# Log-keep sums of a stick-breaking attention: fp32r products of high and low parts in place of fp32 products

## The chip, the core and the metric

The kernel runs on one core of one Trainium2 chip. A core has a matrix engine (TensorE, PE in the profile, with its weight loads listed apart as PEld), three engines for elementwise work (VectorE or DVE, ScalarE or ACT, GpSimd or POOL) and SyncE (SP), which issues most transfers from HBM. Each engine works through its own queue in order and waits for others by semaphores. The metric is the device time of one execution in microseconds. Before the change it is 2654.6 us, the median of 3 runs (2654.39 to 2655.65).

## The reference, cut to what matters

The program is a decoder of two layers over 272 tokens (16 learned ones and 256 of input), width 2048: an RWKV-7 layer with a SwiGLU, then keys and values projected once, then a layer of stick-breaking attention with 16 heads of 128, and a second SwiGLU. The change is in the attention:

```python
z = jnp.einsum('bhqd,bhkd->bhqk', q_blk, k).astype(jnp.float32) * scale
log_keep = jnp.where(valid, -jax.nn.softplus(z), 0.0)
later = lax.cumsum(log_keep, axis=3, reverse=True) - log_keep
weights = jnp.where(valid, jnp.exp(jax.nn.log_sigmoid(z) + later), 0.0)
return jnp.einsum('bhqk,bhkd->bhqd', weights.astype(v.dtype), v)
```

For each query and key, `later` is the sum of the log-keep values of all keys that come after this key (and before the query). The kernel computes these sums as matrix products.

## The kernel before, in words

Activations lie transposed, features on the 128 partitions and tokens along the free axis. Every large projection splits its weights and its activations into a high part, rounded to the narrower type fp32r, and a low part, the remainder, also in fp32r, and adds three products of such parts. Weights stream in through `parts` (lines 152 to 172): SP loads a tile `raw`, ScalarE copies 128x512 of it to `whi` (line 170), VectorE subtracts to get `wlo` (line 171), and six of each may be in flight. In `mm3k` (lines 185 to 194) the matrix engine multiplies them, for the attention's query projection with one matmul of 256 columns (line 193) and one of 512 (line 194) per block of 128 rows.

`attention` (line 987) first makes the keys and values of all 16 heads, then runs `attn_head` (line 1034) for the heads through `interleave` (line 617). That loop takes turns between several heads: `attn_head` is a generator, each `yield` ends a turn, and a new head starts every second turn. The order of instructions on each engine follows from these turns and from the scheduler of the framework, which is free to move instructions within an engine here (the layer before is fixed by hand, the attention isn't).

For one head, `attn_head` does, in this order:

- the query projection, 16 blocks (`mm`, 32 matmuls); then the copy `c` (line 203) on ScalarE and `qx` (lines 204 and 205) on VectorE;
- `head_norm` (line 965): squares `hsq` (line 969), their parts `hs` (lines 971 on ScalarE and 972 on VectorE), two fp32r matmuls `hms` (line 975), an inverse root `hy` and `ht` (lines 978 to 984), and the normed query `q` (line 985);
- the transposed values `tbv` (line 1046) and their copy `vt` (line 1048);
- the scores `z` (line 1054, three fp32 products of 256, 144 and 16 columns);
- on ScalarE and VectorE the log-keep `lk` (lines 1057 to 1062), 128 keys on the partitions by 416 columns of three blocks of keys, and `e`, the log of the sigmoid (line 1063);
- the sums over later keys, `lt` (lines 1065 to 1071);
- `e` plus `lt` (line 1073, VectorE), its exponential (line 1074, ScalarE), the mask (line 1075, VectorE);
- the weighted values `op` (lines 1078 to 1080, three fp32 products), the copy `o` (line 1083) and its parts `hl`.

The sums `lt` take three products that accumulate in one PSUM bank: a triangular matrix of ones times all 416 columns, a full matrix of ones times columns 256 to 400 (144), and the same times columns 400 to 416, written twice (32). The matrices and `lk` are fp32 here, and the profile shows two matmul records for each of the three. GpSimd has no work in the attention: its last work is the recursion for the RWKV layer (lines 1274 to 1281), whose last subtraction starts at 583.6 us.

Of the kernel before, what the change touches and what calls it, by code (L numbers as in the profile page):

```python
# [11 lines left out]
F32 = mybir.dt.float32  # L12
F32R = mybir.dt.float32r
AF = mybir.ActivationFunctionType
ALU = mybir.AluOpType
# [106 lines left out]
class Builder:  # L122
# [864 lines left out]
    def attention(self):  # L987
        tc, nc, a = self.tc, self.nc, self.a
        rs = self.rs
        with ExitStack() as ctx:  # L990
            self.pre = tc.keep_in_program_order(
                nc.scalar.preload_act_table_set("natural_log_exp_and_others"))
            self.at = at = ctx.enter_context(tc.tile_pool(name="at", bufs=2))
            self.ones = at.tile([128, 128], F32R, name="ones", tag="ones", bufs=1)
            nc.scalar.copy(self.ones, self.cst("ones128"))
            Ks, Vs = [], []
            xs = []

            def key_norm(m):
                kv = self.kr.tile([128, 2 * T], F32, name="kv", tag="hl")  # L1000
                k = kv[:, :T]
                Vs.append(kv[:, T:])
                self.head_norm(xs[m], T, self.kgain, k)
                self.dump("K", m, k)
                Ks.append(k)

            first = self.proj_pair((a["sb_w_k"][0], a["sb_w_k"][1]), self.hx2)
            for m in range(NK):
                ps = first[m] if m < 2 else self.proj(a["sb_w_k"][m], self.hx2)
                x = at.tile([128, T], F32, name="kx", tag="kx", bufs=3)  # L1010
                nc.vector.tensor_tensor(x, ps, rs, ALU.mult)
                xs.append(x)
                if m > 0:
                    key_norm(m - 1)
            key_norm(NK - 1)
            for m in range(NK):
                ps = self.proj(a["sb_w_v"][m], self.hx2)
                nc.vector.tensor_tensor(Vs[m], ps, rs, ALU.mult)
                self.dump("V", m, Vs[m])
            os = [None] * NK  # L1020
            self.wide = False
            self.interleave(lambda m: self.attn_head(m, Ks[m], Vs[m], rs, os), ASTRIDE)
            self.wide = True
            acts = []
            for m in range(NK):
                ps = self.proj(a["sb_w_o"][m], os)
                h = self.h[m]
                self.added(h[:, META:], ps)
                self.dump("h3", m, h[:, META:])
                acts.append(self.finish_h(m, META, m == 0, [("g_ffn1", META, self.xs2)])[0])  # L1030
            self.hx = acts
            self.rs = self.norm_rstd(META)

    def attn_head(self, m, K, Vv, rs, os):
        nc, a, at = self.nc, self.a, self.at
        PE, V, A = nc.tensor, nc.vector, nc.scalar
        ps = yield from self.proj_steps(a["sb_w_q"][m], self.hx3, ASTEP)
        x = at.tile([128, T], F32, name="qx", tag="kx", bufs=3)
        self.scaled(x[:, :SEQ], ps, rs[:, META:])
        q = at.tile([128, SEQ], F32, name="q", tag="q")  # L1040
        self.head_norm(x[:, :SEQ], SEQ, self.qgain, q)
        yield 1

        tb = self.pfr.tile([128, 512], F32, name="tbv", tag="fr")
        for i, o in enumerate((0, 128, 144)):
            PE.transpose(tb[:, i * 128:i * 128 + 128], Vv[:, o:o + 128], self.cst("ident"))
        vt = at.tile([128, 384], F32, name="vt", tag="vt")
        A.copy(vt, tb[:, :384])
        parts = ((0, 256, 0, 0), (256, 400, 112, 128), (400, 416, 240, 144))
        yield 1  # L1050
        n = 416
        z = self.psc.tile([128, 512], F32, name="z", tag="sc")
        for c0, c1, q0, k0 in parts:
            PE.matmul(z[:, c0:c1], K[:, k0:k0 + 128], q[:, q0:], start=True, stop=True)  # L1054
        yield 1
        e = at.tile([128, n], F32, name="e", tag="e")
        A.activation(e, z[:, :n], AF.Abs)
        A.activation(e, e, AF.Exp, scale=-1.0)
        A.activation(e, e, AF.Ln, bias=self.one)
        lk = at.tile([128, n], F32, name="lk", tag="lk")  # L1060
        V.scalar_tensor_tensor(lk, z[:, :n], 0.0, e, ALU.max, ALU.add)
        V.tensor_tensor(lk, lk, self.cst("nmask"), ALU.mult)
        V.scalar_tensor_tensor(e, z[:, :n], 0.0, e, ALU.min, ALU.subtract)
        yield 1
        lt = self.psd.tile([128, 512], F32, name="lt", tag="sd")
        tri, ones = self.cst("tri"), self.cst("ones")
        PE.matmul(lt[:, :n], tri, lk, start=True, stop=False)  # L1067
        PE.matmul(lt[:, 112:256], ones, lk[:, 256:400], start=False, stop=False)
        two = lt[:, 112:400].rearrange("p (a t) -> p a t", a=2)[:, :, 128:144]
        PE.matmul(two, ones, lk[:, 400:416].unsqueeze(1).to_broadcast([128, 2, 16]),  # L1070
                  start=False, stop=True)
        yield 1
        V.tensor_tensor(e, e, lt[:, :n], ALU.add)
        A.activation(e, e, AF.Exp)
        V.scalar_tensor_tensor(e, e, -1.0, self.cst("nmask"), ALU.mult, ALU.mult)
        yield 1
        op = self.psd.tile([128, 512], F32, name="op", tag="sd")
        PE.matmul(op[:, :SEQ], vt[:, 0:128], e[:, 0:256], start=True, stop=False)
        PE.matmul(op[:, 112:SEQ], vt[:, 128:256], e[:, 256:400], start=False, stop=False)
        PE.matmul(op[:, 240:SEQ], vt[:, 256:384], e[:, 400:416], start=False, stop=True)  # L1080
        yield 1
        o = at.tile([128, SEQ], F32, name="o", tag="o")
        A.copy(o, op[:, :SEQ])
        self.dump("ao", m, o)
        os[m] = self.split(o, self.xs1)
# [428 lines left out]
```

## Time and profile before

| what | value |
|---|---|
| median of 3 runs | 2654.6 us |
| the profiled execution's own time | 2656.68 us |
| its span, from first to last instruction | 2654.9 us |
| busy in the span: PE, DVE, ACT, POOL | 2641.9, 1787.6, 1490.5, 174.1 us |
| the 16 heads of the attention | about 1684 to 1835 us of the span |
| in these 151 us busy: PE, DVE, ACT, POOL | 151.00, 124.66, 116.62, 0.00 us |
| granted TensorE clock over the span | 1.000 of full |

A row of the timeline gives the start in us from the span's start, the duration in us, the engine, the line of the kernel, the operation, out<-in by tile names with shapes, and how many instructions were merged; a bracket gives the idle time of the engine before the row and what ended it. Matmuls are pipelined, so their durations overlap; what a matmul costs the engine is the time from its start to the next one's start.

### The profile page before, as it was taken

Reading aid. Unit: us, or ns where it says so; the run is one execution under the profiler, and the core shown is the slowest. Engines: PE = TensorE matmul, PEld = TensorE weight load, DVE = VectorE, ACT = ScalarE, POOL = GpSimd, SP = SyncE. Lnnn points to the kernel's source line nnn. Section 1 sums busy time; section 2 is a strip of 40 time slices with the busy share of each in tenths; the row PEclk is TensorE's granted clock in tenths of the full one; section 3 lists DMA queues with packets and bytes.
Section 4 is the critical chain, followed back from the end, with each engine's and each line's share of the span. In section 5 each row is a group of like instructions: output and inputs, shape, how many; then the busy total and the mean of one; then the engine's idle time right before and its main releaser. Section 6 shows DMA issues by size and latency. Waiting matters only on the chain.

```text
span 2654.9 us, 54070 instructions
## 1 busy us (share of the span) xinstructions
PE 2641.9 (100%) x20966; PEld 2455.2 (92%) x20966; DVE 1787.6 (67%) x3618; ACT 1490.5 (56%) x3017; POOL 174.1 (7%) x493
## 2 busy tenths in 40 slices
PE   9999999999999999999999999999999999999999
PEld 8898888889999999999999999888888888888888
DVE  7677777766655555555557775788766666666665
ACT  7775666666544444444446764676555455554553
POOL 0014343440000000000000000000000000000000
PEclk9999999999999999999999999999999999999999
DMA  6434343445555555555555555434555655665655
GB/s 229 145 120 130 96 127 97 124 132 165 174 175 165 186 175 165 185 176 167 184 174 168 181 167 175 143 120 137 189 187 180 197 188 176 201 190 176 199 180 177
DMA packets 186385, 439.54 MB, mean 166 GB/s; under 512 B 58736, under 2 KB 89616, under 8 KB 186128
## 3 DMA queue, kind: packets, MB, share of 16 engines
q1 hardware_dynamic: 184784, 432.90, 51.9%
q8 instruction: 164, 2.69, 0.4%
q0 software_dynamic: 768, 2.23, 0.3%
q10 hardware_dynamic: 576, 0.96, 0.1%
q14 instruction: 93, 0.76, 0.1%
HBM read 430.28 MB, written 5.74 MB: 164 GB/s over the span
## 4 chain that ended last, share of the span: by engine, by line
PE 97%; DMA 1%; ACT 1%; issue 1%; DVE 0%; POOL 0%; SPq 0%; POOLq 0%; ACTq 0%
PE mm L194 23%; PE mm L189 17%; PE mm L191 17%; PE mm L190 17%; PE mm L193 12%; PE lr L587 1%; PE mm L488 1%; PE cb L1426 1%; PE zb L1363 1%; PE yb L1344 1%; PE wa L1374 1%; PE z L1054 1%; PE cb L1418 0%; PE lt L1067 0%; PE ba L1226 0%
## 5 line engine op out<-in xcount | busy, mean ns | idle before, releaser
L171 DVE TENSOR_TENSOR wlo<-raw,whi 128x512 fp32r<-128x512 f32 (+1 forms) x1432 | 968.0, 679 | 596.4 <-ACT whi L170 576.5
L170 ACT CAST whi<-raw 128x512 fp32r<-128x512 f32 (+1 forms) x1432 | 870.3, 610 | 841.2 <-PE mm L190 531.3
L189 PE MATMUL mm<-hl,whi 128*128 128x272 f32 x3328 | 967.2, 291 | 0.0
L191 PE MATMUL mm<-hl,wlo 128*128 128x272 f32 x3328 | 960.4, 289 | 0.0
L190 PE MATMUL mm<-hl,whi 128*128 128x272 f32 x3328 | 958.1, 288 | 0.0
L194 PE MATMUL mm<-hl,whi 128*128 128x512 f32 x2624 | 919.9, 394 | 0.0
L193 PE MATMUL mm<-hl,wlo 128*128 128x256 f32 x2624 | 738.1, 282 | 0.0
L189 PEld LDWEIGHTS mm<-hl,whi 128*128 128x128 f32 x3328 | 625.3, 188 | 10.7 <-issue 8.1
L190 PEld LDWEIGHTS mm<-hl,whi 128*128 128x128 f32 x3328 | 631.2, 190 | 0.0
L191 PEld LDWEIGHTS mm<-hl,wlo 128*128 128x128 f32 x3328 | 625.6, 188 | 0.2
L194 PEld LDWEIGHTS mm<-hl,whi 128*128 128x128 f32 x2624 | 492.4, 188 | 111.9
L193 PEld LDWEIGHTS mm<-hl,wlo 128*128 128x128 f32 x2624 | 494.3, 188 | 0.3
L218 DVE TENSOR_TENSOR wlo<-raw,whi 128x512 fp32r<-128x512 f32 (+2 forms) x156 | 106.6, 691 | 21.7 <-ACT whi L217 19.3
L217 ACT CAST whi<-raw 128x512 fp32r<-128x512 f32 (+2 forms) x156 | 93.1, 609 | 41.4 <-PE mm L190 40.9
L210 DVE TENSOR_TENSOR h<-h,mm 128x256 f32<-128x256 f32 (+1 forms) x224 | 93.9, 420 | 6.6 <-PE mm L194 6.0
L203 ACT COPY c<-mm 128x256 f32<-128x256 f32 x104 | 38.8, 373 | 75.8 <-PE mm L194 75.8
L1281 POOL TENSOR_TENSOR Ts<-Ts,Tm 40x14 f32<-40x14 f32 (+6 forms) x224 | 76.6, 342 | 17.6
L189 PE MATMUL mm<-hi,whi 128*128 128x272 f32 x256 | 75.5, 295 | 0.0
L1279 POOL TENSOR_TENSOR Tm<-Ts,As 40x14 f32<-40x14 f32 (+6 forms) x224 | 74.3, 331 | 17.5
L190 PE MATMUL mm<-lo,whi 128*128 128x272 f32 x256 | 73.8, 288 | 0.0
L191 PE MATMUL mm<-hi,wlo 128*128 128x272 f32 x256 | 73.4, 287 | 0.0
L189 PEld LDWEIGHTS mm<-hi,whi 128*128 128x128 f32 x256 | 48.0, 188 | 1.1
(295 smaller groups left out, 2365.1 us busy)
## 6 DMA issues: line engine op xcount, KB each, us to landing
raw<-w_gate SPq DMA_DIRECT2D x176, 512.0 KB
raw<-w_up SPq DMA_DIRECT2D x176, 512.0 KB
raw<-w_down SPq DMA_DIRECT2D x128, 512.0 KB
raw<-w_down SPq DMA_DIRECT2D x128, 192.0 KB
raw<-w_v SPq DMA_DIRECT2D x32, 512.0 KB
raw<-w_r SPq DMA_DIRECT2D x32, 512.0 KB
raw<-sb_w_k SPq DMA_DIRECT2D x32, 512.0 KB
raw<-sb_w_v SPq DMA_DIRECT2D x32, 512.0 KB
```

Of the source, the lines that this page charges most:

```text
L170: nc.scalar.copy(hi, part)
L171: nc.vector.tensor_tensor(lo, part, hi.bitcast(F32), ALU.subtract)
L189: mm(out, w[0], x[0], start=first, stop=False)
L190: mm(out, w[0], x[1], start=False, stop=False)
L191: return mm(out, w[1], x[0], start=False, stop=last)
L193: mm(out[:, :n], w[1], x[0], start=first, stop=False, skip_group_check=True)
L194: return mm(out, w[0], x[2], start=False, stop=last, skip_group_check=True)
L210: self.nc.vector.tensor_tensor(h, h, out[:, c:c + n], ALU.add)
L217: self.cast = nc.scalar.copy(hi, part)
L218: nc.vector.tensor_tensor(lo, part, hi.bitcast(F32), ALU.subtract)
L1279: V.tensor_tensor(t, Ts[:, 0:i, i:i + 1].to_broadcast([40, i, n]), As[:, i:i + 1, i + 1:].to_broadcast([40, i, n]), ALU.mult)
L1281: V.tensor_tensor(Ts[:, 0:i, i + 1:], Ts[:, 0:i, i + 1:], t, ALU.add)
```

## The change

Two more constant matrices are kept in fp32r: `tri` and `one128`, each made once by a ScalarE copy at the head of `attention`. In `attn_head` the log-keep `lk` is split like the weights are: ScalarE copies it to `lkh` (fp32r), GpSimd subtracts to get `lkl` (fp32r). The three fp32 products become six fp32r products that accumulate in the same bank, the three of `lkh` first, then the three of `lkl`. Two buffers each for `lkh` and `lkl` are added.

```diff
             nc.scalar.copy(self.ones, self.cst("ones128"))
+            self.tri = at.tile([128, 128], F32R, name="tri", tag="tri", bufs=1)
+            self.one128 = at.tile([128, 128], F32R, name="one128", tag="one128", bufs=1)
+            nc.scalar.copy(self.tri, self.cst("tri"))
+            nc.scalar.copy(self.one128, self.cst("ones"))
...
         lk = at.tile([128, n], F32, name="lk", tag="lk")
+        lkh, lkl = (at.tile([128, n], F32R, name=s, tag=s) for s in ("lkh", "lkl"))
         V.scalar_tensor_tensor(lk, z[:, :n], 0.0, e, ALU.max, ALU.add)
         V.tensor_tensor(lk, lk, self.cst("nmask"), ALU.mult)
+        A.copy(lkh, lk)
+        nc.gpsimd.tensor_tensor(lkl, lk, lkh.bitcast(F32), ALU.subtract)
         V.scalar_tensor_tensor(e, z[:, :n], 0.0, e, ALU.min, ALU.subtract)
         yield 1
         lt = self.psd.tile([128, 512], F32, name="lt", tag="sd")
-        tri, ones = self.cst("tri"), self.cst("ones")
-        PE.matmul(lt[:, :n], tri, lk, start=True, stop=False)
-        PE.matmul(lt[:, 112:256], ones, lk[:, 256:400], start=False, stop=False)
         two = lt[:, 112:400].rearrange("p (a t) -> p a t", a=2)[:, :, 128:144]
-        PE.matmul(two, ones, lk[:, 400:416].unsqueeze(1).to_broadcast([128, 2, 16]),
-                  start=False, stop=True)
+        for lk in (lkh, lkl):
+            PE.matmul(lt[:, :n], self.tri, lk, start=lk is lkh, stop=False)
+            PE.matmul(lt[:, 112:256], self.one128, lk[:, 256:400], start=False, stop=False)
+            PE.matmul(two, self.one128, lk[:, 400:416].unsqueeze(1).to_broadcast([128, 2, 16]),
+                      start=False, stop=lk is lkl)
```

The order of instructions shows where the new ones fall. On the matrix engine, in the middle of the 16 heads, before:

```order
L1080 MATMUL op<-e,vt 128x16
L1067 MATMUL lt<-lk,consts_9810 128x416 [waits DVE_49,PE_49]
L1068 MATMUL lt<-lk,consts_9810 128x144
L1070 MATMUL lt<-lk,consts_9810 128x2x16
L1054 MATMUL z<-q,kv 128x256 [waits DVE_49]
```

The same place in the changed kernel:

```order
L1087 MATMUL op<-e,vt 128x16
L1075 MATMUL lt<-lkh,tri 128x416 [waits PE_49,Activation_49]
L1076 MATMUL lt<-lkh,one_20644 128x144
L1077 MATMUL lt<-lkh,one_20644 128x2x16
L1075 MATMUL lt<-lkl,tri 128x416 [waits Pool_49]
L1076 MATMUL lt<-lkl,one_20644 128x144
L1077 MATMUL lt<-lkl,one_20644 128x2x16
L1058 MATMUL z<-q,kv 128x256 [waits DVE_49]
```

The sums stand between the same neighbours, `op` of an earlier head and `z` of a later one; their first product now waits for ScalarE and the fourth for GpSimd, where the first waited for VectorE.

On ScalarE, at the copy that makes `lkh`, before:

```order
L981 ACTIVATE ht<-hy 128x256 [waits Activation_49]
L170 CAST whi<-raw 128x512 [waits DMAHW5_49,PE_49]
L170 CAST whi<-raw 128x512 [waits PE_49]
L203 COPY c<-mm 128x256 [waits PE_49]
L170 CAST whi<-raw 128x512 [waits DMAHW6_49]
```

and in the changed kernel:

```order
L981 ACTIVATE ht<-hy 128x256 [waits Activation_49]
L170 CAST whi<-raw 128x512 [waits DMAHW1_49,PE_49]
L170 CAST whi<-raw 128x512 [waits PE_49]
L1068 CAST lkh<-lk 128x416 [waits DVE_49,Pool_49]
L203 COPY c<-mm 128x256 [waits PE_49]
L170 CAST whi<-raw 128x512 [waits DMAHW2_49]
```

The new copy stands behind two weight copies and ahead of `c`, the copy that follows a query projection.

VectorE gets no instruction and loses none. In the middle of the heads its queue keeps its order, and this is the stretch that runs while `lkh` and `lkl` are made (lines are those of the changed kernel, where 1067 is the mask of `lk` and 1070 the `e` that follows):

```order
L1067 TENSOR_TENSOR lk<-lk,consts_9810 128x416 [waits DVE_49]
L984 SCALAR_TENSOR_TENSOR hy<-hy,dv,ht 128x256 [waits DVE_49]
L1070 SCALAR_TENSOR_TENSOR e<-z,e 128x416
L985 TENSOR_TENSOR q<-qx,hy 128x256 [waits DVE_49]
L204 TENSOR_TENSOR qx<-mm,c 128x256 [waits Activation_49]
L171 TENSOR_TENSOR wlo<-raw,whi 128x512 [waits DMAHW7_49]
L205 TENSOR_TENSOR qx<-qx,rstd 128x256 [waits DVE_49]
```

In every second head the two instructions after the mask stand the other way round, `e` ahead of `hy`, and `qx` (line 204) ahead of `q`. Nothing in it moved. On all engines the order of the last three heads differs somewhat, since the scheduler places their work anew. SP's order is the same row for row.

## The prediction

> **What bounds the kernel now.** I read the page's busy times first, then windows over the attention, then the timelines of single engines there.
>
> ```profile
> PE 2641.9 (100%) x20966; PEld 2455.2 (92%) x20966; DVE 1787.6 (67%) x3618; ACT 1490.5 (56%) x3017; POOL 174.1 (7%) x493
> ```
>
> The matrix engine sets the time over the whole span, and nothing but the attention's 151 us is touched. Two windows (stretch, its length, then busy time and count of PE, PEld, DVE, ACT, POOL, then clock and DMA):
>
> ```profile
> 1707.55:1807.51 99.96, 99.96 (x608) 87.64 (x607) 84.27 (x188) 79.09 (x189) 0.00 (x0) 1.00 0.35 117
> 1817.25:1835.00 17.75, 17.75 (x108) 15.45 (x107) 12.99 (x26) 11.14 (x25) 0.00 (x0) 1.00 0.36 119
> ```
>
> A head has 55 matmul records (32 `mm`, 6 `z`, 6 `lt`, 6 `op`, 3 `tbv`, 2 `hms`), so the first window holds 11 heads of 9.09 us. Per head DVE is busy 84.27/11 = 7.66 us (84%), ACT 7.19 us, GpSimd not at all. The matrix engine is full, but VectorE stands only 1.43 us per head behind it. The second window holds the last heads, where DVE is at 73%. Now the matrix engine in the middle of the heads:
>
> ```profile
> 1754.25 0.28 PE L193 MATMUL mm<-hl,wlo 128*128 128x256 f32 x1
> 1754.37 0.39 PE L194 MATMUL mm<-hl,whi 128*128 128x512 f32 x1
> 1754.60 0.28 PE L193 MATMUL mm<-hl,wlo 128*128 128x256 f32 x1
> ...
> 1760.94 0.94 PE L1067 MATMUL lt<-lk,consts 128*128 128x416 f32 x2
> 1761.73 0.41 PE L1068 MATMUL lt<-lk,consts 128*128 128x144 f32 x2
> 1761.97 0.30 PE L1070 MATMUL lt<-lk,consts 128*128 128x32 f32 x2
> 1762.11 1.05 PE L1054 MATMUL z<-q,kv 128*128 128x256 f32 x6
> ...
> 1830.15 0.36 PE L193 MATMUL mm<-hl,wlo 128*128 128x256 f32 x1
> 1830.36 0.39 PE L194 MATMUL mm<-hl,whi 128*128 128x512 f32 x1
> ```
>
> From start to start, an fp32r product of 256 columns takes 0.12 us and one of 512 takes 0.23. The sums `lt` take 1762.11 - 1760.94 = 1.17 us. Work follows work without a gap.
>
> **What the products save.** By the two fp32r slots, 416 columns take 0.12 + 160/256 x 0.11 = 0.19 us. No fp32r product under 256 columns is in the trace. By columns 144 would take 0.07; for 32 I take the 0.07 of one record of line 1070 (0.14 for two), and 0.09 for the product behind a short one (1830.15 to 1830.36 is 0.21 where 0.12 is usual). New: 2 x (0.09 + 0.19 + 0.07 + 0.07) = 0.84, a saving of 0.33 us per head, 5.3 over 16. Bounds: 0.66 without the two 0.09, a saving of 0.51; and 2 x (0.09 + 0.19 + 0.24 + 0.14) = 1.32 if the narrow ones stay as slow as the fp32 products of lines 1068 and 1070, a loss of 0.15.
>
> **What ScalarE gets.** One cast of 128x416 per head:
>
> ```profile
> 1752.45 0.41 ACT L971 CAST hs<-hsq 128x256 fp32r<-128x256 f32 x1
> ...
> 1755.64 0.55 ACT L1074 ACTIVATE e<-e 128x416 f32<-128x416 f32 x1
> ...
> 1758.95 0.37 ACT L203 COPY c<-mm 128x256 f32<-128x256 f32 x1 [0.90 <-PE mm L194]
> 1759.22 0.62 ACT L170 CAST whi<-raw 128x512 fp32r<-128x512 f32 x1
> ```
>
> Between 0.41 (256 columns) and 0.62 (512) it takes about 0.54 us. It stands right ahead of `c`, in the 0.90 us in which ScalarE waits for the projection; that hides it. Without this cover it would delay `c`, `qx` and `hs` by up to 0.54. ScalarE goes to 7.73 us per head and is no bound. The two casts of constants happen once, each under 0.41 us, while the matrix engine has weights queued: nothing. SP's queue and all DMAs are as before.
>
> **What GpSimd gets, and what it takes from VectorE.** One subtraction of 128x416 from two SBUF inputs per head. The nearest rows are plain two-input ones on 40 partitions:
>
> ```profile
> 306.99 0.73 POOL L1274 TENSOR_TENSOR Ts<-As,consts 40x256 f32<-40x256 f32 x1 [14.26 <-DMA As<-s]
> 307.80 0.21 POOL L1279 TENSOR_TENSOR Tm<-Ts,As 40x14 f32<-40x14 f32 x1
> ```
>
> That is 0.52 us for 242 columns, so 0.73 + 160 x 0.00215 = 1.07 us for 416. None has fp32r output; I take that as equal. Whether 128 partitions cost more isn't shown either. The same rows show what happens when VectorE reads two SBUF inputs at that time:
>
> ```profile
> 411.75 0.68 DVE L218 TENSOR_TENSOR wlo<-raw,whi 128x512 fp32r<-128x512 f32 x1
> ```
>
> ```profile
> 411.77 1.26 POOL L1274 TENSOR_TENSOR Ts<-As,consts 40x256 f32<-40x256 f32 x1 [12.95 <-DMA As<-s]
> ```
>
> ```profile
> 516.88 0.74 POOL L1274 TENSOR_TENSOR Ts<-As,consts 40x256 f32<-40x256 f32 x1 [12.62 <-DMA As<-s]
> ```
>
> ```profile
> 517.19 0.98 DVE L218 TENSOR_TENSOR wlo<-raw,whi 128x512 fp32r<-128x512 f32 x1
> ```
>
> At 411.75 VectorE came first and GpSimd's 0.73 became 1.26: 0.53 more for an overlap of 0.66. At 516.88 GpSimd came first and VectorE's 0.68 became 0.98: 0.30 more for an overlap of 0.43. Whoever comes second waits, for the overlap less 0.13. What VectorE does when `lk` is ready, in the two kinds of heads that alternate:
>
> ```profile
> 1754.36 0.58 DVE L1073 TENSOR_TENSOR e<-e,lt 128x416 f32<-128x416 f32 x1
> 1756.22 0.59 DVE L1075 SCALAR_TENSOR_TENSOR e<-e,consts 128x416 f32<-128x416 f32 x1 [1.27 <-ACT e L1074]
> ...
> 1757.76 0.59 DVE L1062 TENSOR_TENSOR lk<-lk,consts 128x416 f32<-128x416 f32 x1
> 1758.26 0.48 DVE L984 SCALAR_TENSOR_TENSOR hy<-hy,dv,ht 128x256 f32<-128x256 f32 x1
> 1758.66 0.59 DVE L1063 SCALAR_TENSOR_TENSOR e<-z,e 128x416 f32<-128x416 f32 x1
> 1759.16 0.42 DVE L985 TENSOR_TENSOR q<-qx,hy 128x256 f32<-128x256 f32 x1
> ```
>
> ```profile
> 1712.25 0.58 DVE L1062 TENSOR_TENSOR lk<-lk,consts 128x416 f32<-128x416 f32 x1
> ...
> 1713.45 0.48 DVE L984 SCALAR_TENSOR_TENSOR hy<-hy,dv,ht 128x256 f32<-128x256 f32 x1
> 1713.90 0.42 DVE L204 TENSOR_TENSOR qx<-mm,c 128x256 f32<-128x256 f32 x1
> 1714.24 0.42 DVE L985 TENSOR_TENSOR q<-qx,hy 128x256 f32<-128x256 f32 x1
> ```
>
> With 0.03 us per signal: in the first kind `lk` ends at 1758.35, `lkh` runs to 1758.92, GpSimd from 1758.95 to 1760.02. `q` reads two SBUF inputs and would start at 1759.16; it is held 0.86 - 0.13 = 0.73 us. In the second kind `lk` ends at 1712.83 and GpSimd starts at 1713.45, just when `hy` (two SBUF inputs) does. If `hy` is first, GpSimd ends at 1714.87 and `q` loses 0.50; if GpSimd is first, `hy` loses 0.94. I take 0.72. All behind it in VectorE's queue is as late: `q`, `qx`, three `wlo`, then `hs`. `lkl` itself is there in time: `lt` starts almost a microsecond after 1760.02.
>
> VectorE's account per head: 7.66 busy, 0.73 held, and a wait that can't shrink away, since line 1075 needs line 1074, which needs line 1073: 0.55 for line 1074 and two signals, 0.62. Sum 9.01 us against 9.09 now and 8.76 on the matrix engine. VectorE becomes the bound, at -0.08 per head.
>
> A walk along one head ends higher. What is late next is `hs` for `hms`:
>
> ```profile
> 1762.56 0.42 DVE L972 TENSOR_TENSOR hs<-hsq,hs 128x256 fp32r<-128x256 f32 x1
> ```
>
> ```profile
> 1763.67 0.28 PE L975 MATMUL hms<-hs,ones 128*128 128x256 f32 x1
> ```
>
> ```profile
> 1716.71 0.42 DVE L972 TENSOR_TENSOR hs<-hsq,hs 128x256 fp32r<-128x256 f32 x1
> ```
>
> ```profile
> 1717.57 0.48 PE L975 MATMUL hms<-hs,ones 128*128 128x256 f32 x2
> ```
>
> Held by 0.73, `hs` ends at 1763.71, while the matrix engine, 0.33 earlier, wants it at 1763.34: a stall of 0.40 with the signal, +0.07 net. In the other kind (second `hms` 0.12 after the first) `hs` ends at 1717.63 to 1718.07, wanted at 1717.36: stalls of 0.30 to 0.74, -0.03 to +0.41 net. Mean +0.13. Between the account's -0.08 and the walk's +0.13 I take 0 for the 13 heads in which VectorE is this full, and the plain saving for the last three: 3 x 0.33 = 1.0 us.
>
> A rule beside these rows: the Trainium skill (SBUF — State Buffer, section Who interferes with whom) says that a VectorE instruction with two SBUF inputs and a GpSimd instruction that reads SBUF exclude each other and that the second one blocks fully. By that, without my 0.13, the account is 9.14 and the sum 0.3 us below the time before instead of 1.0 below; the rows decide. The Trainium skill (GPSIMD Engine Reference, section 3.1) also has a GpSimd `tensor_tensor` at about 2.6 cycles per element, an estimate of 0.90 us for 416 against my 1.07; by it the account is 8.85 and the sum -4.1 us.
>
> **The rivals.** (a) The hold is absorbed: VectorE idles 1.43 us per head, and if `q`, `hs` and `lk` catch up there, the matrix engine's saving lands whole, 2654.6 - 5.3 = 2649.3 (2646.4 with 0.51 per head). Against it: 1.27 of that idle time stands before line 1075, behind `hms`, where the wait has already happened. (b) GpSimd is slower than its plain rows, by fp32r output or 128 partitions. Above 0.20 + 0.13 us of the operation all is held from VectorE. At 2.05 us (the 1.26 of 411.77 per column) 1.72 are held: 7.66 + 1.72 + 0.62 = 10.00, 13 x 0.91 = +11.8, 2666.4, and no gain at the end. It makes the kernel slower by over 0.2% from about 1.55 us on. The queue's other work speaks for it, no row does. (c) The change saves nothing on the matrix engine, as fp32r products under 256 columns run no faster: +0.15 per head, 16 x 0.15 = +2.4, 2657.0.
>
> **How the numbers follow.** The profiled execution took 2656.68 us, with a span of 2654.9, 2.1 us above the median of the runs; the differences worked out from it go onto the median. Forecast: 2654.6 - 1.0 = 2653.6, its own range 2652.6 (account) to 2656.7 (walk at its worst, 13 x 0.24 - 1.0). Chances: forecast 0.58, (a) 0.15, (b) 0.18, (c) 0.09. A measurement tells about 0.2%, 5.3 us. Faster by more: half of (a) and a little of the forecast's edge, 0.10. Slower by more: nearly all of (b) and an edge, 0.18. Else 0.72. The range takes in (a)'s 2649.3, (c) and the lower part of (b): 2648.5 to 2661.
>
> **What would show it.** Right: POOL rows `lkl` of about 1.1 us; rows of `q` or `hy` on VectorE lengthened by 0.5 to 0.9; VectorE idle well under 1.4 us per head; matrix engine idle before `hms`, by VectorE's or ScalarE's `hs`; `lt` about 0.84 us; a head still about 9.1. Wrong: no lengthened VectorE rows, or heads of 8.8 (a); `lkl` of 1.6 and more, or `lt` waiting for it (b); `lt` of 1.2 and more (c).

## The result, and the profile after

The changed kernel takes 2659.89 us (median of 20 runs, 2657.54 to 2661.75). The kernel before, run beside it, takes 2655.66 us (20 runs, 2652.15 to 2658.24). The ratio is 1.0018 with a 95% interval from 1.0012 to 1.0025: slower by 4.2 us. That is inside the 0.2% that the prediction gave as what can be told from no change, but with 20 runs the interval excludes 1. The forecast was 1.0 us below the time before.

The profiled execution took 2657.54 us. Its span is only 0.8 us longer than that of before, because the untouched work ahead of the attention happened to run 3.3 us shorter in it; so the attention is compared by itself. This is the line of `z`, whose first start is the measure, before and then after:

```profile
L1054 PE MATMUL z<-q,kv x96: 179/286/483, 1690.2 to 1825.2; 128*128 128x256 f32 x32, 128*128 128x144 f32 x32, 128*128 128x16 f32 x32
```

```profile
L1058 PE MATMUL z<-q,kv x96: 179/286/483, 1686.9 to 1824.7; 128*128 128x256 f32 x32, 128*128 128x144 f32 x32, 128*128 128x16 f32 x32
```

The last head's `op` starts at 1832.66 before and at 1833.76 after, on the matrix engine's timeline. From the first `z` to there it was 142.4 us and is now 146.8: +4.4 us, where the medians differ by 4.2. By parts, cut at the starts of `z`: the first four heads +0.5 us, the nine after them +1.4 (0.15 per head), and the last part, from the `z` that starts at 1806.07 on, +2.5 (27.7 us where before it was 25.2).

The last part doesn't hold quite the same work in both. Counted on the timeline, 43 pairs of projection products (256 and 512 columns) lie between its two marks before (1807.51 to 1832.66) and 44 after (1806.07 to 1833.76). The whole program has 2624 pairs in both kernels, and the two parts ahead have equal counts; so one pair, 0.12 + 0.23 = 0.35 us, has moved from behind the last `op` to ahead of it. For equal work the last part is 2.2 us longer, and the attention about 4.1.

Busy times of the whole span after, on the page:

```profile
PE 2640.8 (99%) x20966; PEld 2456.1 (92%) x20966; DVE 1799.5 (68%) x3618; ACT 1501.3 (57%) x3035; POOL 194.9 (7%) x509
```

VectorE has the same 3618 instructions and is busy 11.9 us longer, 0.74 per head. The window over 11 heads (stretch, length, busy time and count of PE, PEld, DVE, ACT, POOL, then clock and DMA):

```profile
1704.58:1806.07 101.49, 99.72 (x609) 88.14 (x607) 91.96 (x188) 86.74 (x200) 13.22 (x11) 1.00 0.35 115
```

A head takes 9.23 us (9.09 before), and the matrix engine is no longer full. VectorE is busy 8.36 us per head, 0.70 more. The rows in the middle of the first kind of head, VectorE and GpSimd, show where it goes:

```profile
1756.72 0.58 DVE L1070 SCALAR_TENSOR_TENSOR e<-z,e 128x416 f32<-128x416 f32 x1
1757.11 1.09 POOL L1069 TENSOR_TENSOR lkl<-lk,lkh 128x416 fp32r<-128x416 f32 x1 [7.82 <-ACT lkh L1068]
1757.22 1.27 DVE L985 TENSOR_TENSOR q<-qx,hy 128x256 f32<-128x256 f32 x1
```

`q` starts 0.11 us after the GpSimd subtraction and takes 1.27 us instead of 0.42. The second kind:

```profile
1766.28 0.47 DVE L984 SCALAR_TENSOR_TENSOR hy<-hy,dv,ht 128x256 f32<-128x256 f32 x1
1766.37 1.34 POOL L1069 TENSOR_TENSOR lkl<-lk,lkh 128x416 fp32r<-128x416 f32 x1 [8.17 <-PE mm L194]
1766.81 0.42 DVE L204 TENSOR_TENSOR qx<-mm,c 128x256 f32<-128x256 f32 x1
1767.15 0.84 DVE L985 TENSOR_TENSOR q<-qx,hy 128x256 f32<-128x256 f32 x1
```

Here `hy` comes 0.09 us first, GpSimd's 1.09 becomes 1.34, and then `q` is held by 0.42. The `qx` between them reads one input from PSUM and keeps its 0.42 us. Over the 11 heads `q` rises from a mean of 416 ns to 1031:

```profile
L985 DVE TENSOR_TENSOR q<-qx,hy 128x256 f32<-128x256 f32 x11 | 11.3, 1031 | 0.0
```

The sums themselves are as short as forecast: each half takes three products, and the matrix engine goes from the first `lt` to `z` in 0.82 us.

```profile
1759.04 0.44 PE L1075 MATMUL lt<-lkh,tri 128*128 128x416 f32 x1
1759.45 0.44 PE L1075 MATMUL lt<-lkl,tri 128*128 128x416 f32 x1
1759.86 1.05 PE L1058 MATMUL z<-q,kv 128*128 128x256 f32 x6
```

What each engine waited for in the 11 heads (total us, times, longest), from the views of waits for PE, ACT and DVE:

```profile
PE hms L975 <- DVE hs L972: 1.6, 6, 0.3
```

```profile
ACT hy L978 <- PE hms L975: 1.8, 6, 0.3
```

```profile
DVE e L1082 <- ACT e L1081: 7.4, 11, 0.7
DVE lk L1066 <- ACT e L1063: 1.8, 6, 0.3
```

In every second head the same 0.3 us goes round: `hs` is late on VectorE, `hms` on the matrix engine, `hy` on ScalarE, and, behind `hy` in ScalarE's queue, the `e` of line 1063, for which VectorE's `lk` then waits. These views count only idle time, and a matmul's modelled end covers some of a wait. From start to start the matrix engine loses time at `hms` in both kinds of head:

```profile
1751.72 0.77 PE L975 MATMUL hms<-hs,ones 128*128 128x256 f32 x2
1752.33 0.27 PE L193 MATMUL mm<-hl,wlo 128*128 128x256 f32 x1
...
1761.40 0.28 PE L193 MATMUL mm<-hl,wlo 128*128 128x256 f32 x1
1761.95 0.39 PE L975 MATMUL hms<-hs,ones 128*128 128x256 f32 x1 [0.27 <-DVE hs L972]
```

The pair of `hms` takes 0.61 us, where it takes 0.32 in the first run below, which has no GpSimd work; it follows the kind of head in which `q` is held by 0.42. In the other kind the product ahead of the second `hms` takes 0.55 us instead of 0.12. From `z` to `z` the two kinds take 9.03 and 9.39 us, and in that run both take 8.74: 0.29 and 0.65 us are lost, nearly all of it at `hms`.

In the last three heads another wait appears, which the kernel before doesn't have:

```profile
1813.05 0.22 PE L1077 MATMUL lt<-lkh,one 128*128 128x32 f32 x1
1813.88 0.45 PE L1075 MATMUL lt<-lkl,tri 128*128 128x416 f32 x1 [0.61 <-POOL lkl L1069]
...
1821.37 0.22 PE L1077 MATMUL lt<-lkh,one 128*128 128x32 f32 x1
1822.52 0.46 PE L1075 MATMUL lt<-lkl,tri 128*128 128x416 f32 x1 [0.93 <-POOL lkl L1069]
...
1830.35 0.22 PE L1077 MATMUL lt<-lkh,one 128*128 128x32 f32 x1
1831.20 0.46 PE L1075 MATMUL lt<-lkl,tri 128*128 128x416 f32 x1 [0.62 <-POOL lkl L1069]
```

The products of `lkh` run there as soon as `lkh` is cast, and the matrix engine then waits for `lkl`. From the last product of `lkh` to the first of `lkl` it takes 0.83, 1.15 and 0.85 us, and in the full heads 0.07 (1759.38 to 1759.45): 2.6 us are lost, of which the view counts 2.2 as idle.

### The profile page after: what moved, and what is told of

It reads as the page before. It is cut to its first block, busy times and chain, and to the rows that moved or that the text cites. A ratio compares the mean times of both kernels' runs of the same rounds, so it can differ in the third digit from the quotient of the medians.

```text
span 2655.7 us, 54137 instructions
## 1 busy us (share of the span) xinstructions
PE 2640.8 (99%) x20966; PEld 2456.1 (92%) x20966; DVE 1799.5 (68%) x3618; ACT 1501.3 (57%) x3035; POOL 194.9 (7%) x509
## 4 chain that ended last, share of the span: by engine, by line
PE 94%; DVE 2%; ACT 1%; issue 1%; POOL 1%; DMA 0%; POOLq 0%; SPq 0%; DVEq 0%; ACTq 0%
PE mm L194 21%; PE mm L189 17%; PE mm L191 17%; PE mm L190 17%; PE mm L193 11%; PE lr L587 1%; PE mm L488 1%; PE cb L1433 1%; PE zb L1370 1%; PE yb L1351 1%; PE wa L1381 1%; DVE wlo L171 1%; PE cb L1425 1%; PE ba L1233 0%; PE hms L975 0%
## 5 line engine op out<-in xcount | busy, mean ns | idle before, releaser
L1069 POOL TENSOR_TENSOR lkl<-lk,lkh 128x416 fp32r<-128x416 f32 x16 | 19.7, 1228 | 1231.0 <-ACT lkh L1068 1198.3
```

## The experiments

The theory: VectorE bounds the full heads because GpSimd's reads of SBUF hold it, and the last three heads lose to the wait for `lkl`. Its rivals: the fp32r products or ScalarE's cast cost the time; or what costs is GpSimd's writing, or its mere presence, and not the subtraction's reading. The kernel before took 2655.24 us beside the first four, 2654.23 beside the last two.

**High part twice, nothing on GpSimd.** The remainder is left out of the sums and the high part multiplied twice, so that the six products and ScalarE's cast stay.

```
-        nc.gpsimd.tensor_tensor(lkl, lk, lkh.bitcast(F32), ALU.subtract)
-        for lk in (lkh, lkl):
+        for i, lk in enumerate((lkh, lkh)):
```

> The changed kernel without GpSimd: the high part takes the place of the remainder in the second three products, so the remainder is left out of the sums. Same six products, same ScalarE cast. Theory (GpSimd's subtraction holds VectorE 0.73 us per head, which makes hs late, and is waited for in the last three heads): heads of 8.76 us, attention 16 x 0.33 = 5.3 us shorter than before, 2655.7 - 5.3 = 2650.4 us, no matrix-engine wait before hms or lt. Rival (the longer chain with the ScalarE cast, or the six products themselves, cost the time): 2656 to 2660.

Measured: 2650.6 us, ratio 0.9983 (0.9974 to 0.9992). The window of 11 heads:

```profile
1707.20:1803.38 96.18, 96.18 (x609) 87.35 (x607) 84.23 (x188) 85.07 (x200) 0.00 (x0) 1.00 0.37 121
```

A head takes 8.74 us; the matrix engine is full again and VectorE back at 7.66. So the saving of the products is real, 0.34 us per head (9.09 to 8.74), and ScalarE's cast costs nothing: the loss is GpSimd's. The last part takes 24.7 us with 44 pairs of projection products, 0.45 less than before with 43, so 0.80 less for equal work.

**The remainder on VectorE.** The computation is whole; one engine's name changes.

```
-        nc.gpsimd.tensor_tensor(lkl, lk, lkh.bitcast(F32), ALU.subtract)
+        V.tensor_tensor(lkl, lk, lkh.bitcast(F32), ALU.subtract)
```

> The remainder is subtracted on VectorE instead of GpSimd, everything else as changed. Theory: 0.50 us of work takes the place of 0.73 us of hold, VectorE's account is 7.66 + 0.50 + 0.62 = 8.78 us per head, just above the matrix engine's 8.76; the last three heads no longer wait over 0.6 us; 2651 to 2653 us. Rival (the length of the chain from lk to lt is what costs): the chain shrinks by half a microsecond only, 2656 to 2658.

Measured: 2651.58 us, ratio 0.9987 (0.9978 to 0.9996), faster than both kernels. The same window:

```profile
1707.03:1803.91 96.88, 96.88 (x608) 87.81 (x607) 90.45 (x200) 85.25 (x199) 0.00 (x0) 1.00 0.37 120
```

```profile
L1069 DVE TENSOR_TENSOR lkl<-lk,lkh x16: 579/584/594, 1696.0 to 1826.0; 128x416 fp32r<-128x416 f32 x16
```

A head takes 8.81 us with the matrix engine full. VectorE does the subtraction in 0.58 us and is busy 8.22 us per head, less than the 8.36 with the subtraction on GpSimd. Taking this work away from VectorE cost VectorE more than doing it. The last part takes 25.4 us with 46 pairs, which for equal work is 0.8 less than before, as in the run above.

**The old products with GpSimd's work kept.** The sums are fp32 products again; the cast and the subtraction run, and nothing reads them.

```
-        for lk in (lkh, lkl):
-            PE.matmul(lt[:, :n], self.tri, lk, start=lk is lkh, stop=False)
+        tri, ones = self.cst("tri"), self.cst("ones")
+        PE.matmul(lt[:, :n], tri, lk, start=True, stop=False)
...
```

> The old fp32 products, with the ScalarE cast and the GpSimd subtraction kept but used by nobody. Theory: VectorE is held 0.73 us per head as in the change, rows of q and hy are lengthened, hs ends 0.73 later against a slack of 0.56 to 0.69, so the matrix engine stalls 0.1 to 0.4 us per head: 2656.5 to 2659.5. Rival (the waits of the products for the parts cost the time, not VectorE): nothing waits for the parts, 2655.7 us.

Measured: 2659.42 us, ratio 1.0018 (1.0009 to 1.0027), as it happens the changed kernel's own ratio.

```profile
1709.65:1811.73 102.08, 101.53 (x608) 87.64 (x607) 91.91 (x189) 86.35 (x201) 13.22 (x11) 1.00 0.35 114
```

A head takes 9.28 us, with VectorE at the same 8.36. The subtraction on GpSimd alone makes the loss of the full heads, and beside it the shorter products are worth 0.05 us per head instead of 0.34. In the last part nothing waits for `lkl`, and it takes 25.6 us, not 27.7. So the attention in this profile is 3.3 us longer than before, where in the change it is 4.4; the medians don't show that difference, and with an interval of 2.4 us either way they can't.

**VectorE for the last three heads only.** The first 13 are as in the change.

```
-        nc.gpsimd.tensor_tensor(lkl, lk, lkh.bitcast(F32), ALU.subtract)
+        (V if m >= 13 else nc.gpsimd).tensor_tensor(lkl, lk, lkh.bitcast(F32), ALU.subtract)
```

> Heads 0 to 12 as changed, the remainder of the last three heads on VectorE. Theory: the part of the loss that lies in the last three heads (2.5 us of 4.4 in the profiles, waits for the remainder of 0.6 to 0.9 us each) goes and turns into their saving of up to 1.0: 2656.4 to 2657.5 us. Rival (the last heads are late only because the heads before them are): 2659.5 to 2660 us.

Measured: 2656.44 us, ratio 1.0007 (0.9998 to 1.0015), which can't be told from the time before; the median lies 1.2 us above it, where the change lies 4.2 above. In the full heads nothing moves:

```profile
1706.10:1807.63 101.53, 99.76 (x608) 88.18 (x607) 91.99 (x188) 86.76 (x200) 13.23 (x11) 1.00 0.36 115
```

That is 9.23 us per head, as in the change. The last part takes 26.2 us instead of 27.7, and no product there waits for `lkl`. It also holds more work, 48 pairs of projection products (1807.63 to 1833.83) instead of 44. Four pairs are 1.4 us, so for equal work the last part is 2.9 us shorter than in the change, and 0.7 shorter than before. That fits the medians, 4.2 and 1.2 us above the kernel before, though each is uncertain by some 2 us. The change thus loses in two places, which add up: VectorE's hold in the full heads, and `lkl` late at the end. Two things end the second loss together and aren't separated: VectorE subtracts in 0.58 us, and the order now has other products between those of `lkh` and of `lkl` (from 1822.12 to 1822.79 in one head).

**GpSimd writes, but doesn't read.** Three fills of `lkl` with zeros stand in for the subtraction, so the remainder is left out of the sums.

```
-        nc.gpsimd.tensor_tensor(lkl, lk, lkh.bitcast(F32), ALU.subtract)
+        for _ in range(3):
+            nc.gpsimd.memset(lkl.bitcast(F32), 0.0)
```

> GpSimd writes the remainder's tile three times with zeros in place of the subtraction, so the remainder is left out of the sums; the six products stay and the fourth still waits for GpSimd. Three writes of 128x416 are about 1.3 us of GpSimd per head (one of 128x325 took 0.37), more than the subtraction's 1.1, but they read nothing from SBUF and needn't wait for lkh. Theory (two readers of SBUF exclude each other): rows of q and hy on VectorE keep 0.42 and 0.48 us, no wait for hs or for the remainder, as without GpSimd: 2650 to 2651.5 us. Rival (any GpSimd work at that time holds VectorE): 2656 to 2660.

Measured: 2650.77 us, ratio 0.9986 (0.9977 to 0.9996). `z` starts every 8.75 us. The fills run behind the products that read `lkl`, at a different place from the subtraction's, but over VectorE instructions of the same kind:

```profile
1758.79 1.89 DVE L171 TENSOR_TENSOR wlo<-raw,whi 128x512 fp32r<-128x512 f32 x3
1760.01 1.45 POOL L1070 MEMSET lkl<- 128x416 f32 x3 [7.29 <-PE lt L1078]
1760.60 0.42 DVE L972 TENSOR_TENSOR hs<-hsq,hs 128x256 fp32r<-128x256 f32 x1
1760.94 0.42 DVE L261 TENSOR_TENSOR hl<-o,hl 128x256 fp32r<-128x256 f32 x1
```

`hs` and `hl` read two SBUF inputs each while GpSimd writes, and keep their 0.42 us. Neither GpSimd's being busy nor its writing is what holds VectorE.

**The subtraction twice.** The second, equal one goes to a tile that nothing reads.

```
         nc.gpsimd.tensor_tensor(lkl, lk, lkh.bitcast(F32), ALU.subtract)
+        lkx = at.tile([128, n], F32R, name="lkx", tag="lkx", bufs=1)
+        nc.gpsimd.tensor_tensor(lkx, lk, lkh.bitcast(F32), ALU.subtract)
```

> The changed kernel with a second, equal GpSimd subtraction per head behind the first, into a tile that nobody reads. Theory: VectorE's busy time grows by another 0.7 to 0.95 us per head (all of it inside rows that already exist), its account is 7.66 + 1.6 + 0.62 = 9.9 us per head, 13 x 0.8 = 10 us for the full heads and the same 2.5 in the last three: 2666 to 2671 us. Rival (the loss comes from waits for the remainder, which is there just as early): 2659.5 to 2660.5.

Measured: 2670.18 us (4 runs), ratio 1.0061 (1.0047 to 1.0074).

```profile
1707.56:1816.74 109.18, 101.06 (x608) 88.53 (x607) 99.63 (x189) 85.61 (x197) 26.56 (x22) 1.00 0.33 107
```

```profile
PE hms L975 <- DVE hs L972: 4.8, 11, 0.6
```

A head takes 9.93 us, 0.70 more than in the change, and VectorE is busy 9.06, again 0.70 more. Each GpSimd subtraction costs VectorE 0.70 us, and the second one lengthens a head by all of it, through `hs` and `hms` as before.

## Why the prediction was wrong

It had the mechanism, and most terms; two steps of its sum failed.

**Terms that held.** The products: 0.84 us forecast, 0.82 measured, so rival (c) falls. ScalarE's cast: 0.54 us, at no cost. GpSimd's subtraction: 1.07 forecast, 1.09 measured where nothing is ahead of it, so rival (b) falls for the full heads. VectorE's hold: 0.73 forecast, 0.70 more busy time measured, of which 0.62 are in `q`. That is an agreement of the mean: in the first kind of head `q` is held by 0.85, where 0.73 was forecast, and in the second by 0.42, where 0.72 was taken as the middle of 0.50 and 0.94. What a second instruction loses is the overlap less about 0.13 us, also here: in the first kind of head `q` overlaps the subtraction by 0.98 us and loses 0.85; in the second, GpSimd overlaps `hy` by 0.38 and loses 0.25, and `q` then overlaps GpSimd by 0.56 and loses 0.42. Of the two orders that the prediction left open in that kind, `hy` first is what happened, in all six such heads of the window. By the Trainium skill (SBUF — State Buffer, section Who interferes with whom) these two kinds of instruction exclude each other; every held row here agrees, and the unheld ones too, as `qx` reads PSUM and the fills read nothing. Read as full blocking, as the prediction read it, it gives 0.13 us too much. The 0.90 us that was estimated from the Trainium skill (GPSIMD Engine Reference, section 3.1) fell short of the 1.09.

**Rival (a), that the hold is absorbed, is out.** The runs without the hold show what the kernel would then have taken: 2650.6 and 2650.77 us, 4.6 and 3.5 below the kernel before beside them, where (a) said 5.3.

**First failed step: "Between the account's -0.08 and the walk's +0.13 I take 0 for the 13 heads".** The walk's +0.13 was close to the +0.14 per head of the window (9.23 against 9.09), but partly by luck. It had a stall of 0.40 us in the first kind and of 0.30 to 0.74 in the second; measured are 0.65 and 0.29, and the two misses cancel in the mean. With `hy` first, as it happened, its own numbers (0.40 and 0.30) give only +0.02. In the first kind the longer hold of `q` is 0.12 of the 0.25 that it missed; the rest isn't worked out. The account was wrong, and the trace of before shows by what. Its waits of VectorE over the 11 heads:

```profile
DVE e L1075 <- ACT e L1074: 14.2, 11, 1.4
DVE lk L1061 <- ACT e L1059: 1.5, 6, 0.2
```

The account kept 0.62 us of the first wait (0.67 is left of it now) and has no term for the second. That one was 0.14 us per head, nearly the difference between the 1.43 us of idle time that the prediction counted and the 1.27 that it placed, and it is 0.16 now: the `e` that it waits for stands behind `hy`, which waits for `hms`, which the hold makes late. As measured, the account reads 7.66 + 0.70 + 0.67 + 0.16 = 9.19, and 0.04 in smaller gaps make the 9.23. Two workings that disagreed should have sent the prediction looking for the missing wait; a middle value was taken instead. Over the first 13 heads this step missed 1.9 us (0.5 + 1.4).

**Second failed step: "the plain saving for the last three", and with it "`lkl` itself is there in time".** The second holds in the full heads, where the subtraction ends at 1758.20 and its product starts at 1759.45. There 2.0 us of projections and `op` stand between the cast's end (1757.04) and the sums. In the last three heads the scheduler puts the sums right behind the cast, which ends at 1812.63, 1820.82 and 1829.94, and the matrix engine waits for `lkl`, 2.6 us in all. Other products stand behind the wait, projections from 1822.96 on among them.

```profile
1812.71 1.12 POOL L1069 TENSOR_TENSOR lkl<-lk,lkh 128x416 fp32r<-128x416 f32 x1 [8.15 <-ACT lkh L1068]
1820.90 1.57 POOL L1069 TENSOR_TENSOR lkl<-lk,lkh 128x416 fp32r<-128x416 f32 x1 [7.07 <-ACT lkh L1068]
1830.01 1.13 POOL L1069 TENSOR_TENSOR lkl<-lk,lkh 128x416 fp32r<-128x416 f32 x1 [7.54 <-ACT lkh L1068]
```

The longest of the three is the one in which two VectorE instructions with two SBUF inputs (`wlo` and `hy`) fall beside the subtraction.

Instead of -1.0 us the last part gives +2.5, or +2.2 for equal work. The plain saving itself is nearly there: without GpSimd the last part gives -0.45, or -0.80 for equal work. The 3.0 us between these two runs, which hold the same products, are the 2.6 of the wait for `lkl` and 0.3 at the pair of `hms` behind the `z` of 1806.07, which still follows a head with the hold (0.63 us instead of 0.32). With VectorE doing the last three subtractions nearly all of it is won back: -0.7 for equal work.

This is the larger error: for equal work 3.2 of the 5.1 us between the forecast's -1.0 and the +4.1 that the attention gained.

**Its signs.** All rows that were to show the mechanism are there. "A head still about 9.1" was off by the first failed step. And "`lt` waiting for it", put down as (b)'s sign, came at the end from the place of the products, with the subtraction at 1.12 and 1.13 us in two of the three cases.

## What to carry to other kernels

Before work is put on an idle GpSimd to spare VectorE, count what its reads of SBUF hold on VectorE: in this kernel 0.70 us per subtraction, while VectorE did the subtraction for 0.56 us of its own time. When an account by engine and a walk along the dependences disagree, list every wait of the engine in the old profile and ask of each whether it can shrink, rather than take a value between. Cost a loop's last rounds apart, since what hides a new step's latency in the middle is other rounds' work, and at the end the order is another. When two runs are compared between two marks, count first whether the same work stands between them.

## What the runs showed of the hardware

It is reading that counts in the hold: a fill of 128x416 by GpSimd takes 0.45 us on the mean and holds nothing (the row below is of the run with fills), while the subtraction of the same size holds `q` on VectorE for 0.85 us in the first kind of head. No run has a GpSimd instruction that reads one input only. And VectorE's own subtraction of 128x416, 0.58 us, is half of GpSimd's 1.09; the 0.70 us that VectorE loses per head is longer than the work that was moved.

```profile
L1070 POOL MEMSET lkl<- 128x416 f32 x42 | 18.7, 445 | 1171.9 <-PE lt L1078 1170.3
```
